# Last 1024 residual columns transposed on TensorE behind the first up blocks; sevens of the last output group five blocks from its end

## The chip, the core and the metric

One core of a Trainium2 chip runs the kernel. Its engines are TensorE (PE; PEld is its weight load), VectorE (DVE), ScalarE (ACT), GpSimd (POOL) and SyncE (SP, which here only issues DMAs). The metric is the device time of one execution in microseconds (us); lower is better. Several runs are timed, and one further execution is profiled; its trace is what is read here.

## The reference

One decoder layer over 256 tokens with model width 2048, all in float32:

```python
h = rms_norm(x, mix_norm_g);  z = h @ w_in            # one projection, split among the heads
x = x + concat([mlstm(z), attention(z)]) @ w_out      # output projection, 2048 x 2048
h = rms_norm(x, ffn_norm_g)
u = h @ w_up;  a, g = split(u)                        # 2048 x 11264
x = x + (gelu(causal_conv3(a)) * g) @ w_down          # 5632 x 2048
x = x + sigmoid(rms_norm(x, ple_norm_g) @ w_ple_gate) * (p @ w_ple_proj)
```

Nearly all of the work is the five weight matrices, each read once from HBM.

## The kernel before

**Products.** TensorE multiplies in the type fp32r. To keep float32 accuracy, every operand is split into a high and a low part (`hi` by a ScalarE cast, `lo` by a VectorE subtraction), and each product is three matmuls: high by high, high by low, low by high (`three`, L360 to L363). The activations stand transposed (features on the 128 partitions, 256 tokens along the row, high part then low part); a weight row block of 128 x 1024 is loaded by SP, split, and used as the moving operand, 512 columns at a time, into PSUM banks.

**Blocks and groups.** The work is a list of blocks, in a fixed order written out by hand. A letter `p` in an order string is a plain block: one row block of the weight matrix, two token tiles by two column halves, 12 matmuls into four banks. The letters `a` and `b` are the four blocks of one "seven" each: two row blocks whose 2 x 2 products are formed by a seven-product scheme, 21 matmuls instead of 24. A seven needs sums of activations made ahead (`sums_of`), sums of its two weight rows on VectorE (L434, L435, L445, L446, or L1745, L1746, L1756, L1757), seven half splits instead of four, and four further banks (`pgP`, `upP`), which are combined after the last seven of the group: `combined` for the output groups (L1060 to L1067, straight into the residual), and L1767 to L1770 for the up groups, into `z_up`.

**Order.** `run_stream` takes the blocks of the input and output projections, `run_units` those that follow. Both load weight rows ahead as buffers come free (three `raw` buffers, some spare tiles), and split up to three or four blocks ahead. A scheduler orders each engine's instructions from that program; `between(hook)` and `behind(hook)` tie a hook's instructions behind given ones on the engines that these run on: `between` behind the last split and load, `behind` behind the instruction that was traced last. All DMAs of one engine's queue are issued in order, so a transfer that waits for its source holds those behind it.

**The seam.** The output projection has two groups of 1024 columns (`out_group`, g_ = 0 and 1). `evac` adds each finished bank to the residual `xs` (L1039). The 11 up groups of 20 or 18 blocks follow (`up_group`, order strings `ORDERS`); they need the residual transposed (`x2T`) with the norm's gain, in high and low parts, row blocks 0 to 15; the norm's scale is applied at the end. The residual is transposed in two steps: VectorE transposes 32 x 32 squares (`square`, L199), 16 DMAs for each 512 columns put the squares in their places (`move`, L205; for every second 512 columns 10 of 16 on SP's queue, else all on GpSimd's), and `column` makes high and low part (L216, L217). For the first output group this happens while the second one runs; for the second output group (columns 1024 to 2047, row blocks 8 to 15) it happens behind the first up blocks, `column` hooked to the up blocks 4 to 7 and 9 to 12. The output group's last two plain blocks are held back and multiplied bank by bank (`hold`), so that the banks are finished one after the other.

Another stage already transposes on TensorE: in the gate group, `transpose_x` (L162) makes row blocks 8 to 15 of the last activations behind that group's first blocks. It transposes two 128 x 128 tiles into a bank by matmuls with the identity (L167) and splits them from there (L158, L159).

Of the kernel before, what the change touches and what calls it, by code (L numbers as in the profile page):

```python
# [9 lines left out]
F32 = mybir.dt.float32  # L10
# [5 lines left out]
P = 128  # L16
# [3 lines left out]
KD = D // P  # L20
# [14 lines left out]
BLK = 1024  # L35
# [8 lines left out]

FRONT = (8, 4, 4)
SEVENS_UP = 2
ORDERS = (*("pppppp" "apapapap" "pppp", "ppp" "apapapap" "bpbpbpb" "pp") * 4,
          *("pppppp" "apapapap" "pppp",) * 3)
START = [sum(map(len, ORDERS[:q])) for q in range(12)]
TURN_AT = (-1, -1, 0, 0)  # L50
GATE_ORDER = "ppppp" "apapapap" "bpbpbb" "p"
OUT_K = (8, 9, 10, 11, 12, 13, 14, 15, 0, 1, 2, 3, 4, 5, 6, 7)
OUT_ORDERS = ("pppp" "apapapap" "bpbpbpb" "p", "ppp" "apapapap" "bpbpbpb" "pp")
ACT_AT = (9, 10, 11, 12, 13, 14, 15, 16, 17, 18)


# [1 line left out]
def layer_kernel(  # L58
# [13 lines left out]
    apool = ctx.enter_context(tc.tile_pool(name="acts", bufs=1))  # L72
# [11 lines left out]
    def bank(tag, name):  # L84
        return ps.tile([P, 512], F32, tag=tag, name=name)

    def f32(ap):
        return ap.bitcast(F32)
# [35 lines left out]
    g_ffn, g_ple, g_ml = vT[:, 0:16], vT[:, 16:32], vT[:, 32:40]  # L124
# [26 lines left out]
    def split_T(dst, src, scale=None):  # L151

        hi, lo = dst[..., 0:256], dst[..., 256:512]
        if scale is None:
            act.copy(hi, src)
            dve.tensor_sub(lo, src, f32(hi))
        else:
            act.activation(hi, src, AF.Copy, scale=scale)  # L158
            dve.scalar_tensor_tensor(out=lo, in0=src, scalar=scale, in1=f32(hi),  # L159
                                     op0=ALU.mult, op1=ALU.subtract)  # L160

    def transpose_x(dst, k0, g, tag="aux"):  # L162

        for k in (k0, k0 + 1):
            bk = bank(tag, f"xT{k}")
            for t in range(NT):
                pe.transpose(bk[:, t * P : (t + 1) * P], xs[:, t, k * P : (k + 1) * P], ident)  # L167
            split_T(dst[:, k, :], bk[:, 0:256], scale=g[:, k : k + 1])

    def sumsq(ssq, c, n):  # L170
        for t in range(NT):
            junk = sm.tile([P, 512], F32, tag="junk", name="junk")[:, :n]
            act.activation(junk, xs[:, t, c * n : (c + 1) * n], AF.Square, accum_out=ssq[:, t, c : c + 1])
# [17 lines left out]
    def squares(name):  # L191

        return mp.tile([P, NT, 4, 128], F32, tag="sq", name=name)
# [7 lines left out]
    def move(y, c, other=None):  # L201

        for a in range(4):
            for b in range(4):
                (other if other and (4 * a + b) % 3 else pool).dma_start(out=c[32 * b : 32 * b + 32, a::4], in_=y[32 * a : 32 * a + 32, :, b])  # L205
# [6 lines left out]
    def column(c, k, dst, gain):  # L212

        src = c[:, :, 32 * k : 32 * k + 32]
        hi, lo = (dst[:, o : o + 256].rearrange("p (a j) -> p a j", j=32) for o in (0, 256))
        act.activation(hi, src, AF.Copy, scale=gain)  # L216
        dve.scalar_tensor_tensor(out=lo, in0=src, scalar=gain, in1=f32(hi), op0=ALU.mult, op1=ALU.subtract)  # L217

    def columns(yz, dst, k0, gain):

        c, start = yz
        while not since(7, start):
            yield
        for k in range(4):
            column(c, k, dst()[:, k0 + k], gain[:, k0 + k : k0 + k + 1])
            yield
# [8 lines left out]
    side = deque()  # L235
    turn = [0]
    rush = []
    done = [0]
# [17 lines left out]
    def since(n, start):  # L256

        return bool(rush) or done[0] >= start + n
# [242 lines left out]
    with mixers:  # L501
# [51 lines left out]
        def evac(dst, c0, n, func=AF.Copy):  # L553
            def f(t, b):
                act.activation(dst()[:, t, c0 : c0 + n], b[:, :n], func, scale=r1["t"][:, t : t + 1])
            return f

        def get(name):
            def f():
                if name not in z:  # L560
                    z[name] = zbuf(name)
                return z[name]
            return f
# [368 lines left out]
        def with_after(b, hook):  # L932
            fn = b.fn
            b.fn = lambda hi, lo: (fn(hi, lo), hook())
# [52 lines left out]
        for c in range(2):  # L987
            f = mv_evac(c)
            add(C_MV + c * 512, 512, after(f, mlstm_out) if c == 1 else f)
        for c in range(2):  # L990
            f = evac(get("mo"), c * 512, 512, AF.Sigmoid)
# [4 lines left out]
        ssq2 = sm.tile([P, NT, 4], F32, name="ssq2")  # L996
# [20 lines left out]
            with_after(blocks[-7 + 3 * r], lambda r=r: out_sums(r))  # L1017
        at_out = len(blocks)
        mk_place = mkT.rearrange("p k s -> p (k s)")
        x2z = {}  # L1020

        def out_group(g_):

            st = {}

            def places(h):
                if g_ == 0 and h == 0:
                    return squares("x2y"), mp.tile([P, NT * 4, 128], F32, tag="col", name="x2z")
                if g_ == 0:
                    v = [mk_place[:, i * BLK : (i + 1) * BLK] for i in range(2)]  # L1030
                else:
                    w = apool.tile([P, 2, BLK], F32, tag=f"aT{1 + h}", name=f"x2w{h}", bufs=2)
                    v = [w[:, i] for i in range(2)]
                return v[0].rearrange("p (t b c) -> p t b c", t=NT, b=4), v[1].rearrange("p (a c) -> p a c", c=P)

            def evac(t, h, o):
                c = 2 * g_ + h
                xc = xs[:, t, c * 512 : (c + 1) * 512]
                dve.tensor_add(xc, o, xc)  # L1039
                if t == 0:  # L1040
                    st[h] = places(h)
                square(st[h][0], t, 0, xc)
                if t == NT - 1:
                    move(*st[h], nc.sync if h else None)

            def added():
                for h in range(2):
                    c = 2 * g_ + h
                    if g_ == 0:
                        side.append(columns((st[h][1], done[0]), get_x2T, c * 4, g_ffn))  # L1050
                    else:
                        x2z[c] = st[h][1]
                    sumsq(ssq2, c, 512)

            def combined(p1, p5, p6, p7):
                c0 = g_ * 1024
                x00, x01, x10, x11 = (xs[:, t, c0 + n * 512 : c0 + (n + 1) * 512] for t in range(NT) for n in range(2))
                right = xs[:, :, c0 + 512 : c0 + 1024]
                a = mqT.rearrange("p g a c -> p (g a c)")[:, g_ * 512 : (g_ + 1) * 512]
                act.copy(a, p1)  # L1060
                dve.tensor_add(x00, p1, x00)
                dve.tensor_add(a, p6, a)
                dve.tensor_add(right, p5.unsqueeze(1).broadcast_to([P, 2, 512]), right)
                dve.tensor_sub(x01, x01, a)
                dve.tensor_add(a, p7, a)
                dve.tensor_add(x10, x10, a)
                dve.tensor_sub(x11, x11, a)  # L1067

            n7 = len(set(OUT_ORDERS[g_]) - {"p"})
            ks = OUT_K if n7 == 2 else (*OUT_K[:2], *OUT_K[4:8], *OUT_K[2:4], *OUT_K[8:])  # L1070
            return pair_group(w_out, lambda: catT, g_ * 1024, 512, OUT_ORDERS[g_], (("mm", "aux"), ("aux", "mm"))[g_],
                              lambda r: S_o["t"][:, r], evac, added, combined, ks, 2 * g_)

        for g_ in range(2):
# [19 lines left out]
    with tc.tile_pool(name="ffn", bufs=1) as fp:  # L1094
        x2 = x2T["t"]
# [589 lines left out]
        def behind(hook):  # L1685
            def f():
                with tc.issue_after(traced()):
                    hook()
            return f

        def between(hook):
            def f():
                with tc.issue_after(last["hi"]), tc.issue_after(last["lo"]), tc.issue_after(last["load"]):
                    hook()
            return f
# [5 lines left out]
        def up_group(q):  # L1701
# [3 lines left out]

            n7 = "a" in ORDERS[q], "b" in ORDERS[q]
            first, n7 = 2 * sum(n7), sum(n7)
# [81 lines left out]
            kinds = {"p": iter(us), "a": iter(seven(0)), "b": iter(seven(1))}  # L1789
            return [next(kinds[c]) for c in ORDERS[q]]  # L1790

# [5 lines left out]
        us = []  # L1797
# [2 lines left out]
        first_late = len(us)  # L1800
        with_after(us[8], between(lambda: keep_x(1)))
        with_after(us[3], between(lambda: r2.update(t=rstd_of(ssq2, "ffn"))))
        for r, i in enumerate((1, 9)):
            with_after(us[i], between(lambda r=r: up_sums(r)))
        for k, i in zip(range(8, KD), (4, 5, 6, 7, 9, 10, 11, 12)):
            with_after(us[i], between(lambda k=k: column(x2z[k // 4], k % 4, x2[:, k], g_ffn[:, k : k + 1])))
        us += down(0, "aux", "mm", sums_done(0), add_rest(0), {}, FIRST, SEVEN[1:])
        us += down(1024, "mm", "aux", sums_done(1024), add_rest(1024),
                   {23: x3_squares(0), 27: x3_squares(1),
# [4 lines left out]
        g_ = gate_pair()  # L1814
# [4 lines left out]
        for c0, n in ((1024, 512), (1536, 512)):  # L1819
            g_ = (units(token_group(w_ple_gate, all_k, get_x3T, c0, n, gate_done(c0, n), tag="aux"))  # L1820
                  if c0 < D - n else last_group(c0, n))
# [44 lines left out]
```

## Time and profile before

| | |
|---|---|
| time, median of 3 runs | 1243.51 us (1243.08 to 1244.33) |
| the profiled execution | 1246.36 us, span from first to last instruction 1244.7 us |
| TensorE | 1227.0 us busy, mean granted clock 0.992 |
| VectorE, ScalarE | 1009.1 us and 757.9 us busy |
| DMA | 277.42 MB, mean 223 GB/s |

A row of the timeline gives start, duration, engine, line, operation, out<-in and shapes, and in brackets how long the engine had been idle before it and what ended that. A row of the windows gives the stretch, its length, busy time and instruction count of PE, PEld, DVE, ACT and POOL, then the granted TensorE clock, the busy share of the DMA engines and GB/s. A row of the chain of waits gives start, duration and what the end of the execution hung on at that time. SPq is SP's queue of DMA issues. Matmuls are pipelined: the recorded duration of one (0.39 us) is longer than the distance between the starts of two.

### The profile page before, as it was taken

The page shows a single profiled execution, that of the slowest core. Times are in us where ns is not written, and L with a number is a line of the kernel's source. Part 1 is how long each engine was busy: PE and PEld are TensorE (multiplying, and loading weights), DVE is VectorE, ACT ScalarE, POOL GpSimd, SP SyncE. Part 2 cuts the span into 40 slices and gives each one's busy share as a digit, 9 for nine tenths or more (in the row PEclk, how much of TensorE's full clock was granted, in tenths as well). Part 3 has the DMA queues.
Part 4 walks back from the last instruction along what each step waited for, and adds up shares of the span by engine and source line. Part 5 has one row for each costly group of instructions (what it writes and reads, how often), then busy time and mean ns, then how long its engine had stood idle before and what let it go on. Part 6 is the DMA issues. An engine that isn't in the chain of part 4 may idle for free.

```text
span 1244.7 us, 16439 instructions
## 1 busy us (share of the span) xinstructions
PE 1227.0 (99%) x5576; PEld 1031.0 (83%) x5576; DVE 1009.1 (81%) x1260; ACT 757.9 (61%) x1107; POOL 185.3 (15%) x343
## 2 busy tenths in 40 slices
PE   9999999999999969999999999999999999999998
PEld 7999988888888848888888887888888888888887
DVE  6888857665689958888988988997797999999773
ACT  7577546464655545865767676666566665556652
POOL 2011247233303031011011101110110000050000
PEclk9999999999999979999999999999999999999999
DMA  8666677776666667776887787767797896886670
GB/s 303 184 197 187 185 216 220 204 211 186 189 199 219 203 202 243 232 233 179 263 257 229 210 253 219 231 207 221 221 317 252 277 356 216 269 254 206 201 227 35
DMA packets 129221, 277.42 MB, mean 223 GB/s; under 512 B 15193, under 2 KB 26193, under 8 KB 129137
## 3 DMA queue, kind: packets, MB, share of 16 engines
q1 hardware_dynamic: 117360, 258.06, 65.5%
q0 software_dynamic: 11392, 18.15, 5.2%
q8 instruction: 44, 0.72, 0.2%
q14 instruction: 40, 0.33, 0.1%
q10 hardware_dynamic: 385, 0.16, 0.1%
HBM read 247.99 MB, written 8.93 MB: 206 GB/s over the span
## 4 chain that ended last, share of the span: by engine, by line
PE 93%; DVE 3%; DMA 2%; issue 1%; ACT 1%; SPq 0%; DVEq 0%; ACTq 0%
PE up L361 11%; PE up L362 11%; PE up L363 11%; PE tg L350 6%; PE tg L351 6%; PE tg L352 6%; PE pg L361 3%; PE pg L362 3%; PE pg L363 3%; PE dnP L1349 1%; PE dnP L1348 1%; PE dnP L1350 1%; PE upP L362 1%; PE upP L363 1%; PE upP L361 1%; PE gt L362 1%
## 5 line engine op out<-in xcount | busy, mean ns | idle before, releaser
L362 PE MATMUL up<-part,x2T 128*128 128x512 f32 x614 | 239.8, 391 | 0.0
L363 PE MATMUL up<-part,x2T 128*128 128x512 f32 x614 | 239.2, 391 | 0.0
L1298 ACT CAST part<-raw 128x1024 fp32r<-128x1024 f32 (+1 forms) x143 | 144.8, 1023 | 113.8 <-PE up L363 27.8
L296 DVE TENSOR_TENSOR lo<-raw,hi 128x1024 fp32r<-128x1024 f32 (+3 forms) x119 | 138.7, 1168 | 78.8 <-ACT hi L294 78.3
L1300 DVE TENSOR_TENSOR part<-raw,part 128x1024 fp32r<-128x1024 f32 (+1 forms) x140 | 164.3, 1182 | 36.8 <-ACT part L1298 28.5
L361 PE MATMUL up<-part,x2T 128*128 128x512 f32 x614 | 188.7, 391 | 1.7 <-ACT x2T L216 1.5
L294 ACT CAST hi<-raw 128x1024 fp32r<-128x1024 f32 (+3 forms) x119 | 119.9, 1009 | 102.6 <-PE tg L352 47.8
L361 PEld LDWEIGHTS up<-part,x2T 128*128 128x128 f32 x614 | 115.9, 189 | 26.9 <-ACT x2T L216 2.3
L362 PEld LDWEIGHTS up<-part,x2T 128*128 128x128 f32 x614 | 116.0, 189 | 24.1
L363 PEld LDWEIGHTS up<-part,x2T 128*128 128x128 f32 x614 | 115.8, 189 | 24.2
L352 PE MATMUL tg<-hi,hT 128*128 128x512 f32 x288 | 113.6, 395 | 0.0
L351 PE MATMUL tg<-lo,hT 128*128 128x512 f32 x288 | 113.3, 393 | 0.0
L350 PE MATMUL tg<-hi,hT 128*128 128x512 f32 x288 | 112.4, 396 | 0.0
L205 POOL DMA_DIRECT2D EZ<-Y x66 | 35.1, 539 | 400.0 <-issue 161.6
L1298 ACT CAST part<-u36r 128x1024 fp32r<-128x1024 f32 (+1 forms) x47 | 48.7, 1035 | 34.8 <-PE up L363 14.8
L1300 DVE TENSOR_TENSOR part<-u36r,part 128x1024 fp32r<-128x1024 f32 (+1 forms) x47 | 56.2, 1198 | 15.5 <-ACT part L1298 14.2
L1298 ACT CAST part<-u32r 128x1024 fp32r<-128x1024 f32 (+1 forms) x42 | 42.9, 1023 | 36.4 <-PE up L363 21.1
L352 PEld LDWEIGHTS tg<-hi,hT 128*128 128x128 f32 x288 | 54.1, 188 | 11.0
L351 PEld LDWEIGHTS tg<-lo,hT 128*128 128x128 f32 x288 | 54.1, 188 | 10.9
L350 PEld LDWEIGHTS tg<-hi,hT 128*128 128x128 f32 x288 | 53.8, 188 | 10.6
L1300 DVE TENSOR_TENSOR part<-u32r,part 128x1024 fp32r<-128x1024 f32 (+1 forms) x42 | 49.6, 1182 | 11.5 <-ACT part L1298 5.9
L362 PE MATMUL pg<-lo,hT 128*128 128x430 f32 (+1 forms) x156 | 55.7, 357 | 0.0
(936 smaller groups left out, 2764.7 us busy)
## 6 DMA issues: line engine op xcount, KB each, us to landing
raw<-in_w_up_dram SPq DMA_DIRECT2D x77, 512.0 KB, 4.7
raw<-in_w_in_dram SPq DMA_DIRECT2D x71, 512.0 KB, 4.4
u36r<-in_w_up_dram SPq DMA_DIRECT2D x43, 512.0 KB, 4.9
raw<-in_w_down_dram SPq DMA_DIRECT2D x41, 512.0 KB, 5.4
u32r<-in_w_up_dram SPq DMA_DIRECT2D x36, 512.0 KB, 5.1
xs<-in_w_up_dram SPq DMA_DIRECT2D x20, 512.0 KB, 5.0
w2b<-in_w_down_dram SPq DMA_DIRECT2D x20, 512.0 KB, 5.0
S<-sums SPq DMA_DIRECT2D x17, 512.0 KB, 4.6
```

Source lines behind the costliest of these rows:

```text
L205: (other if other and (4 * a + b) % 3 else pool).dma_start(out=c[32 * b : 32 * b + 32, a::4], in_=y[32 * a : 32 * a + 32, :, b])
L294: act.copy(hi, raw)
L296: dve.tensor_sub(lo, raw, f32(hi))
L350: pe.matmul(o, ah, hi[:, i, :], start=first, stop=False)
L351: pe.matmul(o, ah, lo[:, i, :], start=False, stop=False)
L352: pe.matmul(o, al, hi[:, i, :], start=False, stop=last)
L361: pe.matmul(o, ah, hi, start=start, stop=False)
L362: pe.matmul(o, ah, lo, start=False, stop=False)
L363: pe.matmul(o, al, hi, start=False, stop=stop)
L1298: act.copy(r32(hi), raw)
L1300: dve.tensor_sub(r32(lo), raw, hi)
L1348: pe.matmul(o, ah, hi, start=first, stop=False)
```

## The change

The second output group no longer makes squares, moves and columns: `evac` returns after the residual add. In their place `transpose_x` is called for row blocks 8 to 15, two at a time, tied behind the up blocks 1, 2, 3 and 4 (before: columns behind the blocks 4 to 7 and 9 to 12). It uses the four banks of the tag `aux`, which the second output group's sums leave and the first up group's sevens take later. In the second output group the two sevens start one block earlier and end five plain blocks before its end (before: two). The first up group has two sevens in place of one (order `pppppp apapapap bpbbbp`, 20 blocks instead of 18), and the following groups alternate one and two; in all there are 16 sevens instead of 15. The sums for the first seven's activations are made one block later. In the first output group the columns are put on the side list at another place in the code, with the same start.

```diff
-ORDERS = (*("pppppp" "apapapap" "pppp", "ppp" "apapapap" "bpbpbpb" "pp") * 4,
-          *("pppppp" "apapapap" "pppp",) * 3)
+ORDERS = ("pppppp" "apapapap" "bpbbbp",
+          *("pppppp" "apapapap" "pppp", "ppp" "apapapap" "bpbpbpb" "pp") * 4,
+          *("pppppp" "apapapap" "pppp",) * 2)
...
-OUT_ORDERS = ("pppp" "apapapap" "bpbpbpb" "p", "ppp" "apapapap" "bpbpbpb" "pp")
+OUT_ORDERS = ("pppp" "apapapap" "bpbpbpb" "p", "pp" "apapapa" "bpbpbb" "ppppp")
...
-        x2z = {}
...
             def places(h):
-                if g_ == 0 and h == 0:
+                if h == 0:
                     return squares("x2y"), mp.tile([P, NT * 4, 128], F32, tag="col", name="x2z")
-                if g_ == 0:
-                    v = [mk_place[:, i * BLK : (i + 1) * BLK] for i in range(2)]
-                else:
-                    w = apool.tile([P, 2, BLK], F32, tag=f"aT{1 + h}", name=f"x2w{h}", bufs=2)
-                    v = [w[:, i] for i in range(2)]
+                v = [mk_place[:, i * BLK : (i + 1) * BLK] for i in range(2)]
                 return v[0].rearrange("p (t b c) -> p t b c", t=NT, b=4), v[1].rearrange("p (a c) -> p a c", c=P)
 
             def evac(t, h, o):
                 c = 2 * g_ + h
                 xc = xs[:, t, c * 512 : (c + 1) * 512]
                 dve.tensor_add(xc, o, xc)
+                if g_:
+                    return
                 if t == 0:
                     st[h] = places(h)
                 square(st[h][0], t, 0, xc)
                 if t == NT - 1:
                     move(*st[h], nc.sync if h else None)
+                    side.append(columns((st[h][1], done[0]), get_x2T, c * 4, g_ffn))
 
             def added():
                 for h in range(2):
-                    c = 2 * g_ + h
-                    if g_ == 0:
-                        side.append(columns((st[h][1], done[0]), get_x2T, c * 4, g_ffn))
-                    else:
-                        x2z[c] = st[h][1]
-                    sumsq(ssq2, c, 512)
+                    sumsq(ssq2, 2 * g_ + h, 512)
...
-        for r, i in enumerate((1, 9)):
+        for r, i in enumerate((2, 9)):
             with_after(us[i], between(lambda r=r: up_sums(r)))
-        for k, i in zip(range(8, KD), (4, 5, 6, 7, 9, 10, 11, 12)):
-            with_after(us[i], between(lambda k=k: column(x2z[k // 4], k % 4, x2[:, k], g_ffn[:, k : k + 1])))
+        for i, k0 in enumerate(range(8, KD, 2)):
+            with_after(us[1 + i], behind(lambda k0=k0: transpose_x(x2, k0, g_ffn)))
```

## The prediction

> **What bounds the kernel now.** I read the page's engine line and its slices first.
>
> ```profile
> PE 1227.0 (99%) x5576; PEld 1031.0 (83%) x5576; DVE 1009.1 (81%) x1260; ACT 757.9 (61%) x1107; POOL 185.3 (15%) x343
> ...
> PE   9999999999999969999999999999999999999998
> ...
> PEclk9999999999999979999999999999999999999999
> ```
>
> TensorE (PE) is busy throughout except in slice 15 (435.6 to 466.7 us), where the granted clock drops too. That slice holds the seam between the last output group and the first up group, which is where the change works. Stretches of 20 us around it, from the windows view (after the busy times: granted clock, DMA share, GB/s):
>
> ```profile
> 424.00:444.00 20.00, 20.00 (x90) 16.58 (x89) 18.75 (x29) 9.84 (x16) 5.39 (x11) 1.00 0.77 231
> 444.00:464.00 20.00, 9.45 (x22) 6.22 (x21) 8.48 (x12) 5.36 (x9) 6.96 (x13) 0.57 0.66 191
> 464.00:484.00 20.00, 20.00 (x89) 16.52 (x88) 15.40 (x20) 11.28 (x14) 0.00 (x0) 1.00 0.79 250
> ```
>
> The seam runs 22 matmuls where its neighbour runs 90: 68 are missing. The TensorE timeline gives the price of one and the parts of the hole:
>
> ```profile
> 444.13 0.39 PE L363 MATMUL upP<-part,x2T 128*128 128x512 f32 x1
> 453.29 1.22 PE L361 MATMUL upP<-part,S_up 128*128 128x512 f32 x2 [8.77 <-ACT part L1298]
> 458.36 0.80 PE L361 MATMUL up<-part,x2T 128*128 128x512 f32 x1 [1.55 <-ACT x2T L216]
> 467.93 1.07 PE L361 MATMUL up<-part,x2T 128*128 128x512 f32 x4
> 468.84 0.39 PE L362 MATMUL up<-part,x2T 128*128 128x512 f32 x1
> ```
>
> At full clock four start in 468.84 - 467.93 = 0.91 us, 0.227 us each, so **the hole costs 68 x 0.227 = 15.4 us**. Of it 8.77 + 1.55 = 10.3 us are idle; the remaining 5.1 us are the slow clock behind the idle time. Who makes the hole is in the chain of waits and in the order of SP's DMA queue (second fence):
>
> ```profile
> 435.25 0.69 DVE x2w L199
> 435.96 9.47 DMA x2w<-x2w
> 446.78 4.44 DMA raw<-in_w_up_dram
> 451.24 1.05 ACT part L1298
> ```
>
> ```profile
> 433.06 1.20 SPq L1275 DMA_DIRECT2D u32r<-in_w_up_dram  x2
> 434.30 1.26 SPq L1275 DMA_DIRECT2D u36r<-in_w_up_dram  x2
> 435.96 10.71 SPq L205 DMA_DIRECT2D x2w<-x2w  x10
> 446.78 1.29 SPq L1275 DMA_DIRECT2D raw<-in_w_up_dram  x2
> ```
>
> Ten square moves of the last output group hold SP's queue from 435.96 to 446.67. The second weight row of the first up seven is issued only behind them; ScalarE (ACT) and VectorE (DVE) wait for it, and TensorE stops. The second idle piece waits for the columns made from the same moved squares (x2T at L216).
>
> **What the change takes away.** The squares, the 16 + 16 moves and the columns of the last 1024 residual columns go. With them the hole goes, if the weight row then comes in time. Its buffer is freed by the split of the fifth up block, and here VectorE is the engine to read:
>
> ```profile
> 433.47 1.25 DVE L1039 TENSOR_TENSOR xs<-pg,xs 128x512 f32<-128x512 f32 x2
> 434.64 1.29 DVE L199 STREAM_TRANSPOSE x2w<-xs 128x512 f32<-128x512 f32 x2
> 435.92 1.23 DVE L1300 TENSOR_TENSOR part<-raw,part 128x1024 fp32r<-128x1024 f32 x1
> 451.24 0.69 DVE L1746 TENSOR_TENSOR raw<-raw,raw 128x512 f32<-128x512 f32 x1 [5.92 <-DMA raw<-in_w_up_dram]
> ```
>
> That split ends at 437.15, and a free queue would issue the row there: landed 4.44 later (the chain's piece) at 441.6, cast 1.05 and split 1.23 later at 443.9, before the block behind 444.13 wants it. The squares (four at 0.65) and part of the combining leave VectorE ahead of this point, so it comes earlier, not later. I take the whole 15.4 us as removed: **-15.4**.
>
> **What it adds: 16 transposes on TensorE.** The same helper runs in the gate group, behind its first blocks as here (its TensorE timeline, then three windows):
>
> ```profile
> 1150.67 0.82 PE L167 MATMUL xT<-ident,xs 128*128 128x128 f32 x6
> 1151.24 0.47 PE L363 MATMUL gt<-part,x3T 128*128 128x512 f32 x1
> ```
>
> ```profile
> 1140.00:1150.00 10.00, 10.00 (x47) 8.19 (x46) 9.39 (x13) 6.39 (x12) 0.68 (x1) 1.00 0.65 241
> 1150.00:1160.00 10.00, 10.00 (x53) 8.28 (x52) 8.16 (x17) 7.38 (x13) 0.77 (x2) 1.00 0.51 166
> 1160.00:1170.00 10.00, 10.00 (x46) 8.25 (x45) 9.33 (x11) 5.37 (x7) 0.00 (x0) 1.00 0.57 164
> ```
>
> Six take 1151.24 - 1150.67 = 0.57 us, 0.095 each; 16 take **+1.5**. TensorE never idles there, at clock 1.00. The Trainium skill (TensorE: Matmul & The Clock Gate, Part 4: PE-mode transpose) speaks against this: about 275 ns for one in a kernel, and the full clock does not engage in it. By its figure 16 would be 4.4 us, an estimate from that page, and the forecast 2.9 us later; the rows above disagree on both, and I go by them. The split of each transposed column (one ScalarE, one VectorE instruction) replaces the same pair of the old columns: 0. No DMA is added on any queue.
>
> **What it moves and adds in sevens.** The first up group has a second seven, one more than before in all (16 instead of 15): 21 products instead of 24 for two rows, 3 x 0.227 = **-0.7**. On VectorE it costs four adds at 0.69 and one and a half splits at 1.23, 4.6 us, which must fit beside TensorE's work. Three places may stall, and no row shows them directly.
>
> (a) Last output group, sevens one block earlier at the front and five blocks from the end instead of two.
>
> ```profile
> 385.20:413.80 28.60, 28.55 (x127) 23.31 (x126) 25.55 (x33) 16.40 (x24) 11.64 (x22) 1.00 0.72 234
> ```
>
> ```profile
> PEld pg L362 <- DVE lo L296: 0.5, 1, 0.5
> ```
>
> Seven plain blocks and two sevens (7 x 12 + 42 matmuls, 28.6 us) now end at 413.8, the group starting at 385.2. In that stretch VectorE works 25.55 us; it must do the last seven's two adds and split (2.6) in it, less one plain split (1.23): 26.9 of 28.6. It fits, tightly; a 0.5 us load stall on a split already shows. Bounds 0 and the 3.05 us that VectorE idles there (if none of that gap can be used). I take 0.5, nearer to the row with TensorE at 28.55.
>
> (b) End of the first up group: one plain block (2.7 us) instead of four blocks follows the last seven, and the next group's banks wait for the combining.
>
> ```profile
> 523.06 0.68 DVE L1768 TENSOR_TENSOR xs<-upP,xs 128x512 f32<-128x512 f32 x1
> 524.79 0.68 DVE L1769 TENSOR_TENSOR xs<-upP,xs 128x512 f32<-128x512 f32 x1
> 527.66 1.22 DVE L1770 TENSOR_TENSOR xs<-upP,xs 128x1024 f32<-128x1024 f32 x1
> ```
>
> ```profile
> 524.00:567.00 43.00, 43.00 (x192) 35.59 (x191) 36.88 (x36) 27.36 (x37) 3.18 (x6) 1.00 0.74 228
> ```
>
> Bare, these three are 2.6 us, hidden under 2.7: 0. Spread among other work, as here in the second up group (two plain blocks, 5.4 us, TensorE never idle), they take 5.8 us, 3.1 more than the cover. The first up group has no earlier group's convolution among them, so I take 0.5.
>
> (c) The transposes queue in order on TensorE ahead of up blocks, and wait for the residual adds (L1039) and for banks that the splits empty. The second and third batch hang behind VectorE and GpSimd instructions, so nothing ties their place on TensorE. The first batch stands behind the second up block, 427.4 + 5.4 = 432.8; the last adds ended at 434.72: up to 1.9 if they stay that late, 0 as in the gate group. The squares that stood between them are gone; 0.5.
>
> **Sum:** -15.4 + 1.5 - 0.7 + 1.5 = **-13.1 us**. The profiled execution took 1246.36 us (span 1244.7) and becomes 1233.3; the median of the runs shown is 2.85 lower: 1243.51 - 13.1 = **1230.4 us**. With no stall 1228.9, with all three at their upper bounds (8.05) 1237.0.
>
> **Rivals.** *VectorE becomes the bound of the seam.* For: 18.75 of 20 us busy before the hole, and 4.6 us more work behind it, with no hole left to catch up in. Against: TensorE ran 20.00 beside it. Stalls of 5 to 8 us: 1234 to 1237, say 1235.5.
>
> *Half the hole stays.* The weight row lands late behind the four loads issued at 433 to 436, and TensorE's order keeps the seven's third part ahead of the plain block, as now.
>
> ```profile
> u36r<-in_w_up_dram SPq DMA_DIRECT2D x2, 512.0 KB, 9.2
> ```
>
> Issued at 437.2 with 9.2 us to land, 446.4; cast and first work at 448.5 as 451.24 to 453.29 now: 4.2 us idle. With the whole slow-clock piece, 5.1, 9.3 us of hole remain: 1239.7. Against: the queue is empty behind those four. The Trainium skill (same page, Why this matters for your kernels) says that an idle gap over about 3 us costs the full clock; the 8.77 us gap agrees.
>
> *It ends slower.* The place is the eight transposed columns, each needing one of four banks: TensorE stops at each until VectorE has emptied one. A cast and a split queued ahead of each (1.05 + 1.23) make 2.3 us, eight times 18.2: 1228.9 + 18.2 = 1247.1. It decides from 14.6 / 8 = 1.8 us a column; the gate group, with the same eight columns, shows none.
>
> *It does not do what it says.* The row stays as late for its buffer as for the queue, and the hole stays whole: 1243.51 + 1.5 - 0.7 = 1244.3. Against: the split that frees it ended 9.6 us before it was issued.
>
> **How the numbers follow.** Forecast 0.68 (own range 1228 to 1234), VectorE bound 0.14, half the hole 0.08, no effect 0.04, slower 0.06. From below, one small idle piece further on might vanish too:
>
> ```profile
> 738.00:780.00 42.00, 41.25 (x181) 33.53 (x180) 36.06 (x40) 28.99 (x40) 3.73 (x7) 1.00 0.69 213
> ```
>
> That is 0.75, so 1228.1, and 0.4 for the spread of the runs: 1227.5 at the low end. At the top 1238.5 takes in the VectorE case with its bound and leaves out the last three (0.18). What differs by under 0.2% (2.5 us) can't be told from no change. Faster: the first three, 0.90; same 0.04; slower 0.06.
>
> **What would show it.** Right: no x2w moves in SP's queue, slice 15 of TensorE at 9 with clock 9, 16 more transposes between 432 and 446 at about 0.1 us, TensorE idle under 2 us between 385 and 490. Step (a) is wrong if TensorE waits for lo at L296 by more than 1 us before 414; (b) if it idles at the second up group's first matmuls on a read of upP; (c) if transposes wait for L1039 or L159. The prediction is wrong if an idle piece over 3 us with a slow clock remains in the seam.

## The result, and the profile after

The changed kernel takes **1231.54 us** (median of 4 runs, 1231.1 to 1232.22); the kernel before, run beside it, took 1243.92 (1243.08 to 1245.41). The ratio is 0.99, with an interval from 0.9883 to 0.9917: 12.4 us faster. The forecast was 1230.4, with a range from 1227.5 to 1238.5. In the profiled executions the span goes from 1244.7 to 1230.4 us.

The page of the changed kernel (engine line, then TensorE's slices and its granted clock):

```profile
PE 1223.2 (99%) x5589; PEld 1030.4 (84%) x5589; DVE 1009.7 (82%) x1262; ACT 757.0 (62%) x1109; POOL 172.9 (14%) x321
...
PE   9999999999999999999999999999999999999998
...
PEclk9999999999999999999999999999999999999999
```

Slice 15 is full and its clock is too. The windows around the seam, and the stretch of the last output group's sevens (stretch, length, busy time of PE, PEld, DVE, ACT, POOL, clock, DMA share, GB/s):

```profile
404.00:424.00 20.00, 19.10 (x84) 15.49 (x84) 18.36 (x24) 13.08 (x18) 3.00 (x6) 1.00 0.66 206
424.00:444.00 20.00, 20.00 (x96) 16.43 (x95) 16.22 (x27) 12.58 (x22) 0.71 (x1) 1.00 0.86 285
444.00:464.00 20.00, 20.00 (x92) 16.59 (x91) 19.06 (x27) 10.49 (x14) 0.00 (x0) 1.00 0.67 205
...
385.20:413.80 28.60, 28.60 (x128) 23.66 (x127) 27.06 (x34) 16.04 (x23) 11.61 (x22) 1.00 0.69 221
```

Where 22 matmuls ran between 444 and 464 there are now 92, four of them transposes, which take the time of nearly two others. A new gap of 0.90 us stands between 404 and 424. The timeline of the changed kernel shows the work that the prediction placed (residual adds, weight rows in SP's queue, the cast of the second weight row, transposes among up blocks):

```profile
429.29 1.88 DVE L1035 TENSOR_TENSOR xs<-pg,xs 128x512 f32<-128x512 f32 x3
432.33 7.62 SPq L1269 DMA_DIRECT2D raw<-in_w_up_dram  x3
441.10 1.05 ACT L1292 CAST part<-raw 128x1024 fp32r<-128x1024 f32 x1 [0.74 <-DMA raw<-in_w_up_dram]
436.81 0.60 PE L168 MATMUL xT<-ident,xs 128*128 128x128 f32 x4
437.17 0.48 PE L362 MATMUL up<-part,x2T 128*128 128x512 f32 x1
415.53 0.96 PE L362 MATMUL pg<-hi,catT 128*128 128x512 f32 x3 [0.90 <-ACT hi L295]
```

No square moves stand in SP's queue there any more. The last residual adds end at 431.2, where they ended at 434.7 before. Four transposes take 437.17 - 436.81 = 0.36 us, 0.09 each. The last row is the only idle piece of TensorE between 385 and 500 us. What that one waits for is told by SP's queue and by the chain of waits:

```profile
395.88 6.50 SPq L206 DMA_DIRECT2D mkT<-mkT  x10
402.47 0.53 SPq L286 DMA_DIRECT2D raw<-in_w_out_dram  x1
404.24 4.94 SPq L286 DMA_DIRECT2D raw<-in_w_out_dram  x2
```

```profile
403.08 1.14 DVE lo L297
404.24 9.14 DMA raw<-in_w_out_dram
```

Ten moves of the *first* output group hold SP's queue until 402.4. Three loads follow them there, and behind these a weight row of the second group, which is issued at 404.24 and lands 9.14 later. The chain names a VectorE split as what released it: that split frees the row's buffer. So the row itself left the queue as soon as it had a place; what was late is its landing.

The spans add up: -15.4 for the hole, -0.75 for a piece idle at 738 to 780 before that is gone too, +0.9 for the new gap, +1.5 for the transposes and -0.7 for the seven give -14.45; the difference is -14.3. The profiled execution of before lay 2.4 above its median and that of the changed kernel 0.7 above its own, so that the medians differ by less.

### The profile page after: what moved, and what is told of

Its sections match the earlier page's. It is cut to its first block, busy times and chain, and to the rows that moved or that the text cites. A ratio compares the mean times of both kernels' runs of the same rounds, so it can differ in the third digit from the quotient of the medians.

```text
span 1230.4 us, 16417 instructions
## 1 busy us (share of the span) xinstructions
PE 1223.2 (99%) x5589; PEld 1030.4 (84%) x5589; DVE 1009.7 (82%) x1262; ACT 757.0 (62%) x1109; POOL 172.9 (14%) x321
## 4 chain that ended last, share of the span: by engine, by line
PE 96%; DMA 1%; DVE 1%; issue 0%; ACT 0%; SPq 0%; ACTq 0%; DVEq 0%
PE up L364 12%; PE up L362 12%; PE up L363 11%; PE tg L351 6%; PE tg L352 6%; PE tg L353 6%; PE pg L362 4%; PE pg L363 4%; PE pg L364 4%; PE dnP L1342 1%; PE dnP L1344 1%; PE dnP L1343 1%; PE upP L363 1%; PE upP L364 1%; PE upP L362 1%; PE gt L363 1%
## 5 line engine op out<-in xcount | busy, mean ns | idle before, releaser
L363 PE MATMUL up<-part,x2T 128*128 128x512 f32 x608 | 237.0, 390 | 0.0
L364 PE MATMUL up<-part,x2T 128*128 128x512 f32 x608 | 236.6, 390 | 0.0
L362 PE MATMUL up<-part,x2T 128*128 128x512 f32 x608 | 185.6, 390 | 0.0
L363 PEld LDWEIGHTS up<-part,x2T 128*128 128x128 f32 x608 | 114.2, 188 | 23.6
L364 PEld LDWEIGHTS up<-part,x2T 128*128 128x128 f32 x608 | 114.2, 188 | 23.5
L362 PEld LDWEIGHTS up<-part,x2T 128*128 128x128 f32 x608 | 114.2, 188 | 23.6
```

The lines of the kernel that those rows point to most:

```text
L362: pe.matmul(o, ah, hi, start=start, stop=False)
L363: pe.matmul(o, ah, lo, start=False, stop=False)
L364: pe.matmul(o, al, hi, start=False, stop=stop)
```

## The experiments

In the diffs a minus is the changed kernel, unless they say otherwise. Times are medians; each ratio is against runs of the kernel before on the same chip (1245.08 for the two kernels that undo one half each and the two that put the moves back, 1245.67 for the others). The span of the profiled execution is given too. A difference of spans rests on one execution of each kernel: the wait for the first load of `x` alone is between 0 and 2.0 us in them.

### The transposes without the new orders

```diff
-ORDERS = ("pppppp" "apapapap" "bpbbbp",
-          *("pppppp" "apapapap" "pppp", "ppp" "apapapap" "bpbpbpb" "pp") * 4,
-          *("pppppp" "apapapap" "pppp",) * 2)
+ORDERS = (*("pppppp" "apapapap" "pppp", "ppp" "apapapap" "bpbpbpb" "pp") * 4,
+          *("pppppp" "apapapap" "pppp",) * 3)
-OUT_ORDERS = ("pppp" "apapapap" "bpbpbpb" "p", "pp" "apapapa" "bpbpbb" "ppppp")
+OUT_ORDERS = ("pppp" "apapapap" "bpbpbpb" "p", "ppp" "apapapap" "bpbpbpb" "pp")
```

> The changed kernel with both order strings of before: only the squares, moves and columns are replaced by transposes on TensorE. Theory A (the moves' hold on SP's queue and the late columns made the hole, the transposes take it away): 1231 to 1232 us, 0.7 more than the changed kernel for the missing seven and 0.9 less for the stall at 415.5 in the last output group. Rival B (the orders took the hole away, by relieving VectorE at the seam): 1238 us or more, with an idle piece of over 3 us between 430 and 470.

Measured: 1236.79 us, ratio 0.9935 (0.9921 to 0.995), span 1235.4: 8.3 us faster, and neither number. The hole at 444 is gone, and a new one has come at the end of the first up group. From the timeline of this kernel:

```profile
439.50 0.83 ACT L158 ACTIVATE x2T<-xT,vT 128x256 fp32r<-128x256 f32 x2
443.84 1.05 ACT L1291 CAST part<-raw 128x1024 fp32r<-128x1024 f32 x1 [2.78 <-DMA raw<-in_w_up_dram]
461.61 0.69 DVE L1762 TENSOR_TENSOR xs<-upP,xs 128x512 f32<-128x512 f32 x1
464.47 1.22 DVE L1293 TENSOR_TENSOR part<-raw,part 128x1024 fp32r<-128x1024 f32 x1
462.68 1.19 PE L361 MATMUL up<-part,x2T 128*128 128x512 f32 x4 [1.22 <-ACT part L1291]
465.74 0.51 PE L362 MATMUL up<-part,x2T 128*128 128x512 f32 x1 [1.87 <-DVE part L1293]
```

```profile
460.00:480.00 20.00, 16.90 (x67) 13.22 (x66) 12.10 (x12) 9.45 (x12) 0.00 (x0) 0.91 0.83 278
```

TensorE loses 90 - 67 = 23 matmuls there, 5.2 us: 3.1 idle and the rest a slow clock. The split that it waits for ends at 465.7, as the last of a row of VectorE's work that has no gap from 444.9 on. So the removal of squares, moves and columns takes the hole away and gives a third of it back later in the same group: 15.4 - 5.2 - 1.5 for the transposes is 8.7, near the 8.3 measured.

### The new output order without the transposes

The edit is against the kernel before:

```diff
-OUT_ORDERS = ("pppp" "apapapap" "bpbpbpb" "p", "ppp" "apapapap" "bpbpbpb" "pp")
+OUT_ORDERS = ("pppp" "apapapap" "bpbpbpb" "p", "pp" "apapapa" "bpbpbb" "ppppp")
```

> The kernel before with the changed order of the last output group alone; squares, moves and columns stay. Theory A: the hole stays, 1243 to 1245 us, with ten moves in SP's queue ahead of the weight row. Rival B: the hole is mostly gone, 1231 to 1237 us.

Measured: 1240.32 us, ratio 0.9954 (0.9937 to 0.9971), span 1239.8: 4.8 us faster, and neither number (one of the four runs took 1236.95). Its timeline:

```profile
433.29 2.86 SPq L1275 DMA_DIRECT2D raw<-in_w_up_dram  x2
436.84 8.90 SPq L205 DMA_DIRECT2D x2w<-x2w  x10
448.31 1.08 PE L361 MATMUL upP<-part,S_up 128*128 128x512 f32 x2 [2.61 <-ACT part L1298]
453.39 0.80 PE L361 MATMUL up<-part,x2T 128*128 128x512 f32 x1 [1.54 <-ACT x2T L216]
443.93 1.05 ACT L1298 CAST part<-raw 128x1024 fp32r<-128x1024 f32 x1 [1.01 <-DMA raw<-in_w_up_dram]
452.83 2.10 ACT L216 ACTIVATE x2T<-x2w,vT 128x256 fp32r<-128x256 f32 x5
```

```profile
444.00:464.00 20.00, 15.46 (x50) 11.10 (x49) 12.82 (x19) 9.97 (x14) 5.99 (x11) 0.74 0.57 165
```

The weight rows, which stood behind the ten moves before, are now issued ahead of them: their buffers come free earlier, because the residual adds and the combining are done earlier. The 8.77 us of idle time become 2.61 here. The second piece, the wait for the columns, stays at 1.54, as expected of a kernel that still has the moves. So the order takes a third of the time of the hole by itself, and the prediction had costed it as a small loss. In the seam it brings 28 of the 68 matmuls back, 6.4 us, and a gap of 1.41 us at 415 takes a part of that again.

Forty matmuls are still missing with the row ahead of the moves, so the queue isn't the whole cause. Set this kernel beside the one with the transposes alone. The seven's second row lands at nearly the same time in both (its cast starts at 443.93 here and at 443.84 there), and the one stops while the other does not. What differs is the columns. The first six plain blocks of the up group use row blocks 2 to 7; every later one needs a row block from 8 on. ScalarE starts on the first of these columns at 439.50 there and at 452.83 here. With the transposes TensorE works without a pause until the seven's sums come, at 449.2; with the moves it runs out of plain blocks after the sixth, and stops from 445.70 to 448.31. Both kernels differ in the output order too, and no run has the transposes with the row behind the moves. How the hole of the kernel before divides between the late row and the late columns is therefore not shown.

### Both, without the new seven; and the new seven with the old output order

```diff
-ORDERS = ("pppppp" "apapapap" "bpbbbp",
-          *("pppppp" "apapapap" "pppp", "ppp" "apapapap" "bpbpbpb" "pp") * 4,
-          *("pppppp" "apapapap" "pppp",) * 2)
+ORDERS = (*("pppppp" "apapapap" "pppp", "ppp" "apapapap" "bpbpbpb" "pp") * 4,
+          *("pppppp" "apapapap" "pppp",) * 3)
```

> The changed kernel with the up orders of before, 15 sevens. Theory A: 0.7 us slower than the changed kernel (three matmuls at 0.227), 1232.2 us. Rival F (the second seven of the first up group is paid for on VectorE): no slower, 1231.5 us or less.

Measured: 1232.86 us, ratio 0.9896 (0.9883 to 0.991), span 1231.4. In the seam TensorE waits once, 1.33 us at 415.5. The span is 1.0 above that of the changed kernel, 0.4 of it that wait, so that some 0.6 are left for the seven, where its three products are 0.7. That is theory A's price, but the ratios of the two can't be told apart. With the two runs above this is a square of four: the transposes alone 0.65%, the order alone 0.46%, and both 1.04%, about their sum (1.11%).

The other corner is the changed kernel with the old order of the last output group:

```diff
-OUT_ORDERS = ("pppp" "apapapap" "bpbpbpb" "p", "pp" "apapapa" "bpbpbb" "ppppp")
+OUT_ORDERS = ("pppp" "apapapap" "bpbpbpb" "p", "ppp" "apapapap" "bpbpbpb" "pp")
```

> The changed kernel with the last output group's order of before (sevens two blocks from its end). Theory A (the new order is worth nothing by itself and costs the 0.9 us stall at 415.5): 1230.5 to 1231.5 us. Rival E (the five plain blocks give VectorE the room that the seam needs, now that columns 8 are wanted four up blocks in): 1233 to 1237 us, with TensorE waiting for VectorE or for the first transposes around 430 to 445.

Measured: 1234.5 us, ratio 0.991 (0.9894 to 0.9925), span 1232.4. Its waits of TensorE in the seam and one row of its VectorE timeline:

```profile
PE up L362 <- ACT x2T L159: 0.6, 1, 0.6
PE upP L362 <- DVE x2T L160: 0.5, 1, 0.5
PE xT L168 <- DVE x2T L160: 0.4, 1, 0.4
```

```profile
472.33 0.69 DVE L1762 TENSOR_TENSOR xs<-upP,xs 128x512 f32<-128x512 f32 x1 [0.59 <-PE upP L364]
```

These are the waits that the prediction's step (c) feared: with the residual adds late, transposes and their splits come late by 0.4 to 0.6 us each, and the trace favours rival E. With the new order none is left. What the new order is worth beside two sevens is 2.0 us by the spans (0.6 of it a longer wait for the first load of `x`), 1.2 by the ratios and 3.0 by the medians. The intervals of the ratios overlap widely. By the trace it removes 1.5 us of waits and adds the 0.9 us at 415, so a gain is likely, and its size is open. And the stall at 462 of the transposes alone is absent, though the output order is the same: with two sevens in the first up group the combining stands behind the second one, and its add runs at 472.33 instead of 461.61, out of the way of the splits. The new seven so does more than save its three products, if the output order is the old one.

### What holds the row: the moves put back, unused

The squares and the moves of the last 1024 columns are made again, in addition, and nothing reads them; ten go on SP's queue as before:

```diff
+                if g_:
+                    w = apool.tile([P, 2, BLK], F32, tag=f"aT{1 + h}", name=f"x2w{h}", bufs=2)
+                    return w[:, 0].rearrange("p (t b c) -> p t b c", t=NT, b=4), w[:, 1].rearrange("p (a c) -> p a c", c=P)
...
-                if g_:
-                    return
...
-                if t == NT - 1:
+                if t == NT - 1 and g_:
+                    move(*st[h], nc.sync if h else None)
+                elif t == NT - 1:
```

> The changed kernel, and the last output group makes its squares and 32 moves as before too, ten of them on SP's queue; nothing reads them. Theory A (the hold on the queue by itself stops TensorE): weight rows land up to 10 us late, an idle piece of 4 to 9 us with slow clock behind it, 1238 to 1246 us. Rival C (only the late columns mattered, the queue was hidden anyway): 1231 to 1234 us, the squares on VectorE at 2.6 us being the only price.

Measured: 1234.41 us, ratio 0.9913 (0.9898 to 0.9928), span 1233.6. In its SP queue the moves hold 9.3 us, as before, but again behind the weight rows:

```profile
435.65 2.86 SPq L1272 DMA_DIRECT2D raw<-in_w_up_dram  x2
438.87 9.31 SPq L206 DMA_DIRECT2D x2w<-x2w  x10
```

TensorE has no idle piece in the seam. Of the 3.2 us that this span lies above the changed kernel's, 2.6 are there before the seam (the first output group's ten moves start at 398.48 instead of 395.88; 1.2 of it is a longer wait for the first load of `x`), and 0.55 is a wait at 713, so the seam itself costs nothing that can be seen. Theory A (the hold on SP's queue makes the hole, whatever else is changed) expected far more, and falls in this form. Rival C (only the late columns mattered) said 1231 to 1234 us and is missed by 0.4. The second edit is the same with all the moves on GpSimd's queue, `move(*st[h], None)` in place of `move(*st[h], nc.sync if h else None)`:

> As the run before, but all 32 dead moves on GpSimd's queue, none on SP's. Theory A: 1231.5 to 1233 us, no idle piece over 1 us at the seam. Rival D (the traffic of the moves on the DMA engines or the squares on VectorE stop TensorE, whichever queue issues them): as slow as with SP's queue, 1238 us or more.

Measured: 1232.12 us, ratio 0.9899 (0.9884 to 0.9913), span 1230.8, which is the changed kernel within what can be told. So four squares on VectorE and 32 moves cost nothing here that can be told; that rules rival D out. Taken together: the moves do no harm where the needed row is ahead of them *and* the columns come from the transposes. Both hold in these two runs, so they do not tell rival C from a hold that harms only the rows *behind* it. In the kernel before, the old output order put the row behind the moves and the columns came from them; the change took away both.

### What stalls TensorE at 462

The stall of the transposes alone ended on VectorE, which was full. This edit, against that kernel, moves the sums of row blocks for the next group's second seven (2.3 us on VectorE) five blocks later. The expectation below calls them a part of the output group's combining; they are `up_sums`, sums of the transposed residual:

```diff
-        for r, i in enumerate((2, 9)):
+        for r, i in enumerate((2, 14)):
```

> The kernel with the transposes alone (both orders of the sevens as before), with the second part of the last output group's combining hooked to the fifteenth entry of the up list in place of the tenth, so that VectorE is spared some of its work ahead of the first up group's last seven. Theory V (the stall at 462.7 there is a backlog of VectorE): the idle 3.1 us at 462-466 shrinks to under 1.5 and the clock stays at 1.00: 1232-1234.5, where the transposes alone took 1236.8. Rival Y (the stall is a weight row that lands late): the idle piece stays as it is, 1236-1238. If the combining holds up something else when later (banks of the first up group), a new idle piece shows on a read of upP or xs and the time is 1236 or more with the old piece gone.

Measured: 1238.21 us, ratio 0.9941 (0.9927 to 0.9955), span 1236.5. The stall has grown, though VectorE has gaps before it. Its timeline and its chain of waits:

```profile
462.61 0.69 DVE L1762 TENSOR_TENSOR xs<-upP,xs 128x512 f32<-128x512 f32 x1 [1.48 <-DMA kept_x<-xs]
464.35 0.68 DVE L1787 TENSOR_TENSOR EZ<-x2T 128x512 f32<-128x512 f32 x1
467.35 0.79 PE L362 MATMUL up<-part,x2T 128*128 128x512 f32 x1 [3.48 <-DVE part L1293]
```

```profile
453.93 8.56 DMA kept_x<-xs
```

VectorE's combining add writes into `xs`, and that place must first have been saved by the copy `kept_x<-xs`. The copy lands 8.56 us after its issue; the add stands in front of splits in VectorE's queue and makes them wait. Theory V's number falls, and so does a late weight row (Y). The moved sums did not help: the first of them now runs at 464.35, between the add and the split that TensorE waits for. In the kernel with the transposes alone the copy was issued at 453.2 and took 8.0 us, to 461.2, and the add ran at 461.61, 0.4 us later. There VectorE's backlog ends last, with the copy 0.4 us ahead of it, so that easing VectorE alone can bring little; which of them is worth more in that kernel is not settled by these runs.

### The slow clock behind the hole

The prediction took 5.1 of the 15.4 us as slow clock that idle time brings. The edit puts products that nobody uses into the hole of the kernel before:

```diff
+        def keep_warm():
+            bk = bank("aux", "warm2")
+            for _ in range(34):
+                pe.matmul(bk, x2[:, 0, 0:P], x2[:, 1, :], start=True, stop=True)
+
+        with_after(us[6], behind(keep_warm))
```

> The kernel before with 34 extra products of 128x512 (fp32r, result unused, in a spare bank) queued on TensorE behind the fifth up block, where the hole of the seam lies: 34 x 0.227 = 7.7 us of work in an idle piece of 8.77 us. Theory W (the 5.1 us of the hole that I did not find as idle time are a slow clock that the idle time brings): with the idle piece filled TensorE's clock stays at 1.00, the first products after the hole run at 0.23 us each, and the time falls by about 5, to 1238.5-1240.5. Rival X (the slow clock of the seam comes from somewhere else, such as the DMA traffic or the program's place): the cadence behind the hole stays slow and the time stays within 1 us of before, or is later by what the extra products overrun the hole.

Measured: 1241.12 us, ratio 0.9971 (0.9958 to 0.9985), span 1239.4. The time falls by 3.6 us by the ratio and the span by 5.3, with 7.7 us of work *added* (28 of the 34 products ran in the hole, six just before it). Window and timeline:

```profile
444.00:464.00 20.00, 16.46 (x70) 12.70 (x69) 11.10 (x14) 8.05 (x12) 6.55 (x13) 1.00 0.62 186
```

```profile
445.11 6.51 PE L1810 MATMUL warm<-x2T 128*128 128x512 f32 x28
453.09 0.73 PE L361 MATMUL upP<-part,S_up 128*128 128x512 f32 x2 [1.47 <-ACT part L1298]
457.10 0.50 PE L361 MATMUL up<-part,x2T 128*128 128x512 f32 x1 [1.54 <-ACT x2T L216]
```

The weight row is as late as before, but the clock is 1.00 where it was 0.57, and 70 - 28 = 42 useful matmuls fit where 22 did. Theory W holds (its range is missed by 0.6, with runs of the kernel before that are 2.2 above those it started from), and the split of the hole into idle time and slow clock is shown, not only argued.

### What a transpose costs

```diff
-    def transpose_x(dst, k0, g, tag="aux"):
+    def transpose_x(dst, k0, g, tag="aux", twice=1):
...
-            for t in range(NT):
+            for t in [*range(NT)] * twice:
...
-            with_after(us[1 + i], behind(lambda k0=k0: transpose_x(x2, k0, g_ffn)))
+            with_after(us[1 + i], behind(lambda k0=k0: transpose_x(x2, k0, g_ffn, twice=2)))
```

> The changed kernel with each of the 16 transposes at the seam made twice into the same place. Theory A: 16 more at 0.095 us, 1.5 us slower, 1233.0 us, clock as before. Rival G (a transpose costs TensorE about 0.275 us, its own recorded duration, or slows the clock): 4 us slower or more, 1235.5 us.

Measured: 1233.83 us, ratio 0.9907 (0.9893 to 0.992), span 1232.1, 1.7 us more than the changed kernel (2.3 by the medians, 0.9 by the ratios), for 16 more transposes of which 16 x 0.095 = 1.5. That is theory A; rival G wanted 4 or more. The windows of this kernel:

```profile
424.00:444.00 20.00, 20.00 (x100) 16.56 (x99) 15.94 (x27) 11.81 (x22) 0.29 (x1) 1.00 0.83 283
444.00:464.00 20.00, 20.00 (x96) 16.57 (x95) 18.25 (x27) 11.20 (x14) 0.41 (x1) 1.00 0.65 188
```

Even 32 of them leave TensorE full and its clock at 1.00. By the Trainium skill (TensorE: Matmul & The Clock Gate, Part 4: PE-mode transpose) the added 16 would be 4.4 us, an estimate from its 275 ns; the 1.7 us disagree with it for transposes that stand among longer products, as here. Whether transposes by themselves would hold the full clock is not shown by any run.

### The gap that is left, at 415

All moves of the first output group go to GpSimd's queue:

```diff
-                    move(*st[h], nc.sync if h else None)
+                    move(*st[h])
```

> The changed kernel with the first output group's moves all on GpSimd's queue, where ten of them hold SP's at 395.9 to 402.4. Theory A (the 0.9 us stall at 415.5 is a weight row held behind these moves): no such stall, 1230.6 us. Rival H (the stall comes from VectorE or ScalarE being late): 1231.5 us, the stall stays.

Measured: 1236.45 us, ratio 0.9929 (0.9915 to 0.9942), span 1234.7. Neither number is met. The gap at 415 is gone, so the moves on SP's queue did make it, but not by holding that row: it is issued at 403.78, as before right behind the VectorE split that frees its buffer, and is cast at 410.00, at most 6.2 us later, where it took 9.14. What the moves held were the three loads ahead of it. In place of the gap TensorE waits for the columns, which the moves on one queue make late; from the timeline:

```profile
430.36 0.80 PE L362 MATMUL up<-part,x2T 128*128 128x512 f32 x1 [3.73 <-ACT x2T L217]
```

Half of it: five moves on SP's queue instead of ten. (The row that the expectation gives to the first up group is one of the output projection, `in_w_out`.)

```diff
-    def move(y, c, other=None):
+    def move(y, c, other=None, only=0):
...
-                (other if other and (4 * a + b) % 3 else pool).dma_start(out=c[32 * b : 32 * b + 32, a::4], in_=y[32 * a : 32 * a + 32, :, b])
+                (other if other and (4 * a + b) % 3 and (4 * a + b) % 3 != only else pool).dma_start(out=c[32 * b : 32 * b + 32, a::4], in_=y[32 * a : 32 * a + 32, :, b])
...
-                    move(*st[h], nc.sync if h else None)
+                    move(*st[h], nc.sync if h else None, 1)
```

> The changed kernel with five of the first output group's second-half moves on SP's queue, and eleven on GpSimd's, where it is ten and six. Theory M (the 0.9 us stall at 415.5 is a weight row of the first up group held behind these ten moves): SP's queue is free some 3 us earlier, the stall at 415.5 goes, and the time is 1231.54 - 0.9 = 1230.6, if the columns do not get late. Rival N (GpSimd's five more moves make the columns late, as with all sixteen on GpSimd, where TensorE waited 3.73 us at 430): a wait on x2T of 0.5 to 2 us near 425-431: 1231.5-1234.

Measured: 1231.87 us, ratio 0.9887 (0.9873 to 0.9901), span 1229.9. From its waits of TensorE:

```profile
PE up L364 <- DVE x2T L218: 0.3, 1, 0.3
```

The gap at 415 is gone and 0.3 us of waiting for a column has come: M and N are both right in part, and the time is in N's range. The span is 0.5 shorter than that of the changed kernel and the ratio lower by 0.0013, with intervals that overlap almost wholly. Whether this version beats the changed kernel stays open.

### Two sevens more

```diff
-          *("pppppp" "apapapap" "pppp",) * 2)
+          *("ppp" "apapapap" "bpbpbpb" "pp",) * 2)
```

> The changed kernel with two sevens in each of the last two up groups, where they have one: 18 sevens in all in place of 16. Theory S (TensorE is the bound there, VectorE has room: a seven is worth its three products, 0.7 us, or the 1.3 that the seven of the first up group measured): 1231.54 - 1.4 = 1230.1, down to 1229. Rival T (VectorE, with 4.6 us more for each seven, is late for the end of the up groups and the gate group's start): idle pieces on part or on sums behind the last up groups, 1231.5-1236.

Measured: 1243.95 us, ratio 0.9987 (0.9978 to 0.9996), span 1241.9: nearly all of the gain is lost, and rival T is right beyond its own range. Timeline, chain and window of this kernel:

```profile
868.80 6.58 SPq L206 DMA_DIRECT2D EZ<-Y  x10
875.47 2.69 SPq L1269 DMA_DIRECT2D raw<-in_w_up_dram  x3
882.19 1.59 PE L362 MATMUL up<-part,x2T 128*128 128x512 f32 x4 [1.99 <-ACT part L1292]
884.04 0.63 PE L364 MATMUL up<-part,x2T 128*128 128x512 f32 x1
884.47 0.63 PE L363 MATMUL up<-part,x2T 128*128 128x512 f32 x1
889.15 1.19 PE L362 MATMUL up<-part,x2T 128*128 128x512 f32 x4 [1.62 <-ACT part L1292]
903.88 1.20 PE L362 MATMUL up<-part,x2T 128*128 128x512 f32 x4 [1.83 <-ACT part L1292]
```

```profile
875.47 5.53 DMA raw<-in_w_up_dram
```

```profile
880.00:900.00 20.00, 16.32 (x62) 12.33 (x62) 13.55 (x14) 13.21 (x21) 0.00 (x0) 0.91 0.69 227
```

It is the seam's pattern once more, in the middle of the up groups: VectorE runs without a gap from 846 to 872, its splits free the buffers late, ten moves of squares (here of the up products) stand in SP's queue up to 875.38, the row is issued at 875.47 and lands 5.53 later, TensorE idles and its clock drops. The chain names VectorE's splits ahead of that row (from 873.57 on), and the moves end 0.09 us before its issue, so which of the two held it longer is not shown. Between 880 and 900 28 matmuls of 90 are missing, 6.4 us. Here VectorE had no room for a seven's 4.6 us, and its 0.7 us were lost many times over.

## Why the prediction was right, and where not

**The hole, -15.4: right in sum, wrong in whom it credits.** Of the 68 missing matmuls 66 are back, and four transposes take the place of the others. The row landed at 441.1 (said: 441.6), its split ended at 445.8 instead of 443.9 behind sums on VectorE, and no product waited for it. But the step said that squares, moves and columns take the hole with them, and alone they bring 8.3 us. The prediction had a stall of about that size in the VectorE rival, "no hole left to catch up in", and the transposes alone show one (VectorE 19.08 of 20 us busy between 444 and 464, the stall at 462), with the copy of `xs` as a second limit that ends 0.4 us earlier. In the change as a whole it does not appear: one_seven_less and old_out_order show that either of the two orders keeps it away. The sum had neither this stall of 5.2 us nor the gain of the output order; that they cancel is luck. The step also made the row the cause of 8.77 of the 10.3 idle us. out_order_alone shows that a row issued ahead of the moves still leaves 40 matmuls missing while the columns are late.

**(a) The last output group's order, +0.5: wrong sign.** VectorE's 27.06 us of 28.60 met the working's 26.9, and no product waited for `lo`. The 0.90 us that appeared at 415 come from a weight row that lands late behind the first group's moves, so the size was near for a wrong reason. What the step left out is what the order does *behind* it: the combining and the last residual adds leave VectorE 3.5 us earlier, the up rows' buffers come free earlier, and their loads get ahead of anything else in SP's queue. That is 4.8 us alone, 4.0 with the transposes (by the spans 1235.4 and 1231.4), and with the seven too some 1 to 3 that the intervals do not settle. The row stood in the prediction: the adds at 433.47 with the split that frees the buffer behind them.

**(b) and (c), +0.5 each: nothing.** No idle piece of TensorE shows between 416.5 and 523 us. For (c), old_out_order shows 1.5 us of such waits if the adds are late; the first transpose ran at 433.59.

**Transposes and seven: right.** 0.09 us each against 0.095 (on the clock the gate group's rows could say little, with six transposes in a row at most), no wait on the banks; the "slower" rival (2.3 us for each column) has nothing in the trace. The seven's -0.7 fits the spans but is too small to be told by times.

**The clock, 5.1: right**, by warm_hole. The first term of the range's low end, the 0.75 us at 738 to 780, did vanish. Two small slips change nothing: 1228.1 - 0.4 is 1227.7, not 1227.5, and the idle piece of "half the hole" is 4.0 us, from 444.5 to 448.5, not 4.2.

The forecast came out 1.1 us low: 0.4 is the median of before (1243.92 in this comparison, 1243.51 in the runs shown), 0.7 the difference (12.4 instead of 13.1). In the profiled spans the difference was 14.3, larger than the sum by the stalls (0.9 instead of 1.5) and the 0.75.

## What to carry to other kernels

A transfer in an in-order queue costs what stands behind it, and whether something needed stands behind it is decided by when its buffer came free. So when a stall is traced to a queue, ask what holds it, why the needed transfer was late to join, and why the waiting engine had no other work; each may be moved, and here the late row and the late columns came from the same moves. A change to the order of the work is not to be costed only in the stretch in which it lies: follow the buffers that it frees to the next stage. And before adding work to an engine that is off the critical path, look at what its instructions free.

## What the runs showed of the hardware that was not expected

**Idle pieces under 3 us can cost the full clock.** The Trainium skill (TensorE: Matmul & The Clock Gate, Why this matters for your kernels) puts the limit at about 3 us. In these traces matmuls started every 0.43 us, instead of 0.227, behind one piece of 1.99 us (884.04 and 884.47 with two sevens more), behind 2.61 us with the output order alone, and behind 1.87 us that came 1.2 us of work after a piece of 1.22 with the transposes alone. They kept the pace behind single pieces of 1.62 and 1.83 us, and behind 1.47, 0.53 and 1.54 us within 5.5 us (warm_hole). For single pieces the limit in these few cases lies between 1.83 and 1.99 us; what else enters into it the runs do not show.

**Here a gap was cheaper filled than empty.** 7.7 us of useless products at the hole shortened the kernel by 3.6 us (1.9 to 5.2 by the interval).
